# Second attention: the scores of both halves of the heads emitted ahead of their softmax, upper and lower rows of the array in turn

## The chip, the cores and the metric

The kernel runs on one core of a Trainium2 chip. The metric is the device time of one execution in microseconds (us); lower is better. TensorE is called PE in the profile, its weight loads PEld, VectorE DVE, ScalarE ACT, GpSimd POOL and SyncE SP.

## The reference, cut to what matters

Two blocks of two layers each run one after the other on 256 tokens of width 1024, in float32. The first block has two layers of a gated delta rule with an HGRN2 scan and a gated feed-forward network; the second has one layer of sparse attention and one of sliding-window attention, each followed by a convolutional feed-forward network. The change lies in the second attention alone, which is this:

```python
def swa_sink_mixer(h, k, v, w_q, sinks, w_out):
    ...
    sc = jnp.einsum('bnqgrd,bnkgd->bgrnqk', qb, kk).astype(jnp.float32) * (HEAD_DIM ** -0.5)
    ...
    sc = jnp.where(mask, sc, NEG)
    ...
    mx = jnp.maximum(sc.max(axis=-1, keepdims=True), sink)
    e = jnp.exp(sc - mx)
    p = e / (e.sum(axis=-1, keepdims=True) + jnp.exp(sink - mx))
    o = jnp.einsum('bgrnqk,bnkgd->bnqgrd', p.astype(vv.dtype), vv)
    return o.reshape(b, s, N_HEADS * HEAD_DIM) @ w_out
```

There are 16 query heads of 64 channels and 2 key heads. A query attends to the 128 positions up to its own. Each row of scores gets a learned sink value that takes part in the maximum and in the sum.

## The kernel before, in words

Activations lie channel by channel: partition p of chunk k is channel 128k+p, and the 256 tokens run along the free axis. Every large projection is three fp32r matmuls per weight tile (lines 185 to 187), on weights that ACT and DVE split in two as they arrive (lines 176 and 177).

The second attention is `_swa`. `SWA_ORDER` writes its steps out by hand: "q0 q1 q2 k0 u1 u3 q3 u0 u2 u5 u4 j0 u6 u7 j1 j2 j3". A "q" step projects four query heads, "k0" the keys and values, a "u" step is one unit of attention (`swa_unit`), a "j" step brings a quarter of the result back to channel-major form (`channel_major`, line 967), and `proj_out` follows.

There are eight units. Unit u(2n+c) takes four heads (two chunks r = 0, 1 of the query tile, and in each a lower half of the partitions, hf = 0, and an upper half, hf = 1) and the 128 queries of chunk c. Units with c = 1 (u1, u3, u5, u7) score 256 keys, those with c = 0 (u0, u2, u4, u6) 128. In what follows they are the wide and the narrow units. For one unit the code emits, for hf = 0 and then for hf = 1:

- a PSUM tile `sc` for the scores (line 1250, from `scores`, two buffers under the tag "sc") and two score matmuls, r = 0 and r = 1 (line 1252). They contract over 64 partitions, so each uses one half of the rows of the array; in float32 each is two passes in the trace, with a weight load each;
- the softmax in `softmax_rows`: two DVE instructions that add the mask and find the row maximum (line 951), two exponentials on ACT (through `act`, line 269), the transposes of the result through PE into a tile of the tag "px" (line 957; four for a wide unit, two for a narrow one, for each half), and one copy to `ptb` on ACT (line 959);
- the matmuls with the values into `po` (line 1257; four or two float32 matmuls for each half, two passes each). `po` has a single buffer.

After both halves come the sink's terms and the scaling into `ot` (lines 1259 to 1263).

The order in which instructions stand on an engine is not the order in which the code emits them. The build sorts them: an instruction is placed on its engine when, by the build's own plan, its inputs are there and its buffer is free, and among several that could go the one that was emitted first goes. So emission order is a priority. The trace shows this: scores of a later unit stand between the transposes of an earlier one.

The two lines that the change takes apart:

```python
for r in range(2):
    nc.tensor.matmul(sv[:, r * nk : (r + 1) * nk], q[a, 2 * n + r, c * P : (c + 1) * P], kt[a, 0, :nk], start=True, stop=True)
```

Of the kernel before, what the change touches and what calls it, by code (L numbers as in the profile page):

```python
# [16 lines left out]
P = 128  # L17
# [87 lines left out]
class K:  # L105
# [1136 lines left out]
    def swa_unit(self, n, c, q, kt, vv, nsk, ot):  # L1242
        nc = self.nc
        nk = (c + 1) * P
        sk = self.c("sink")
        st = self.sp.tile([P, 2, 8], F32, name="st", tag="st", bufs=4)
        po = self.psn.tile([P, 512], F32, name="po", tag="pn")
        for hf in range(2):
            a = slice(64 * hf, 64 * hf + 64)
            sv = self.scores()  # L1250
            for r in range(2):
                nc.tensor.matmul(sv[:, r * nk : (r + 1) * nk], q[a, 2 * n + r, c * P : (c + 1) * P], kt[a, 0, :nk], start=True, stop=True)  # L1252
            idx = [2 * r + hf for r in range(2)]
            ptb = self.softmax_rows(sv, self.c("bandcau") if c else self.c("cau"), [nsk[:, 4 * n + i : 4 * n + i + 1] for i in idx], st, idx, c)
            for r, u in enumerate(idx):
                for k in range(c + 1):
                    nc.tensor.matmul(po[:, 64 * u : 64 * u + 64], ptb[:, r * (c + 1) + k], vv[:, k, 64 * hf : 64 * hf + 64], start=k == 0, stop=k == c)  # L1257
        rr = self.sp.tile([P, 8], F32, name="rr", tag="rr", bufs=4)
        nc.vector.tensor_add(rr[:, :4], st[:, 0, :4], sk[:, 4 * n : 4 * n + 4])
        self.act(rr[:, :4], rr[:, :4], AF.Exp)  # L1260
        nc.vector.tensor_add(rr[:, :4], rr[:, :4], st[:, 1, :4])
        nc.vector.reciprocal(rr[:, 4:], rr[:, :4])
        nc.vector.tensor_mul(
            ot[:, c, n * 256 : (n + 1) * 256].rearrange("p (u d) -> p u d", d=64),
            po[:, :256].rearrange("p (u d) -> p u d", d=64),
            rr[:, 4:].rearrange("p (u o) -> p u o", o=1).to_broadcast([P, 4, 64]),
        )
# [175 lines left out]
```

## Time and profile before

| | |
|---|---|
| median of three runs | 1612.43 us (1607.37 to 1614.89) |
| the profiled execution | 1614.79 us, its span 1613.0 us |
| mean granted clock of TensorE | 0.987 of 2.4 GHz |
| PE busy | 1559.1 us, 97% of the span |
| DVE, ACT, POOL busy | 1191.5, 978.3 and 260.4 us (74%, 61%, 16%) |
| scores of the second attention (line 1252) | from 1351.6 to 1383 us of the span |

PE is busy nearly all the time, but a busy PE need not be a full one: matmuls are pipelined, the ends of their records are modelled, and waits inside the array count as busy. So the distance from one start to the next says more than the busy share. In the timeline a row merges instructions of one line that follow without a gap; the columns are start, length in us, engine, line, operation, tiles, shape and count, and in brackets the idle time before it with what ended it.

### The profile page before, as it was taken

How to read it: one execution, taken by the hardware profiler on the slowest of the kernel's cores; microseconds unless marked ns; L12 is line 12 of the kernel's file. 1: busy time of each engine (PE TensorE's matmuls, PEld its weight loads, DVE VectorE, ACT ScalarE, POOL GpSimd, SP SyncE). 2: the span in 40 equal slices, each digit the busy share in tenths (PEclk: the TensorE clock that was granted, in tenths of full speed). 3: DMA queues.
4: the chain of work that ended last, by engine and by line, in shares of the span. 5: the costliest groups of instructions: out<-in, count | busy, mean ns of one | idle time of the engine just before them, and what ended most of it. 6: DMA issues, size and time to landing. Idle time of an engine off the chain costs nothing.

```text
span 1613.0 us, 37688 instructions
## 1 busy us (share of the span) xinstructions
PE 1559.1 (97%) x15418; PEld 1497.6 (93%) x15418; DVE 1191.5 (74%) x2178; ACT 978.3 (61%) x1707; POOL 260.4 (16%) x243
## 2 busy tenths in 40 slices
PE   8999999999999989899999999999999999999997
PEld 8888889999999979789999998998999997999997
DVE  7795848777667885757777768786888667688853
ACT  7756755555546848574655554776666555666653
POOL 1021101122211201101122121003222100123210
PEclk9999999999999999999999999999999999999999
DMA  6542425566664532416655565532556654256562
GB/s 208 183 119 68 137 63 183 172 188 189 175 192 147 171 123 79 132 53 205 203 189 188 174 193 166 175 92 66 183 185 186 182 183 147 79 180 187 184 177 86
DMA packets 73436, 249.60 MB, mean 155 GB/s; under 512 B 10768, under 2 KB 11184, under 8 KB 73264
## 3 DMA queue, kind: packets, MB, share of 16 engines
q1 hardware_dynamic: 70752, 245.65, 49.1%
q8 instruction: 121, 1.98, 0.5%
q10 hardware_dynamic: 2512, 1.55, 0.3%
q14 instruction: 51, 0.42, 0.1%
HBM read 243.34 MB, written 1.06 MB: 152 GB/s over the span
## 4 chain that ended last, share of the span: by engine, by line
PE 48%; DVE 2%; ACT 1%; issue 1%; DMA 0%; POOL 0%; SPq 0%; ACTq 0%; DVEq 0%
PE pu L185 9%; PE pu L187 9%; PE pu L186 9%; PE pa L185 4%; PE pa L186 4%; PE pa L187 4%; PE po L1069 1%; PE ps L957 1%; PE po L185 1%; PE po L186 1%; PE po L187 1%; DVE wlo L177 1%; PE sc L1252 1%; PE po L1257 1%; ACT whi L176 1%
## 5 line engine op out<-in xcount | busy, mean ns | idle before, releaser
L176 ACT CAST whi<-raw 128x1024 fp32r<-128x1024 f32 (+1 forms) x462 | 475.5, 1034 | 435.1 <-PE pu L186 264.8
L177 DVE TENSOR_TENSOR wlo<-raw,whi 128x1024 fp32r<-128x1024 f32 (+1 forms) x462 | 564.7, 1226 | 180.1 <-ACT whi L176 179.1
L185 PE MATMUL pu<-xh,whi 128*128 128x256 f32 x2368 | 671.4, 284 | 8.7 <-issue 3.8
L187 PE MATMUL pu<-xh,wlo 128*128 128x256 f32 x2368 | 671.6, 284 | 5.0 <-DVE wlo L177 5.0
L186 PE MATMUL pu<-xl,whi 128*128 128x256 f32 x2368 | 670.9, 283 | 0.0
L185 PEld LDWEIGHTS pu<-xh,whi 128*128 128x128 f32 x2368 | 447.4, 189 | 12.4 <-issue 6.1
L187 PEld LDWEIGHTS pu<-xh,wlo 128*128 128x128 f32 x2368 | 447.9, 189 | 9.4 <-DVE wlo L177 6.0
L186 PEld LDWEIGHTS pu<-xl,whi 128*128 128x128 f32 x2368 | 448.2, 189 | 4.8 <-issue 3.3
L185 PE MATMUL pa<-ah,whi 128*128 128x256 f32 x704 | 197.1, 280 | 0.0
L186 PE MATMUL pa<-al,whi 128*128 128x256 f32 x704 | 196.7, 279 | 0.0
L187 PE MATMUL pa<-ah,wlo 128*128 128x256 f32 x704 | 196.7, 279 | 0.0
L186 PEld LDWEIGHTS pa<-al,whi 128*128 128x128 f32 x704 | 132.1, 188 | 0.0
L187 PEld LDWEIGHTS pa<-ah,wlo 128*128 128x128 f32 x704 | 132.0, 188 | 0.0
L185 PEld LDWEIGHTS pa<-ah,whi 128*128 128x128 f32 x704 | 132.0, 188 | 0.0
L360 POOL TENSOR_TENSOR sg<-sg,cu 128x256 f32<-128x256 f32 x44 | 71.6, 1628 | 196.5 <-DVE al L339 159.2
L360 POOL TENSOR_TENSOR sg<-sg,gu 128x256 f32<-128x256 f32 x44 | 61.1, 1388 | 204.1 <-ACT sg L269 204.1
L350 DVE TENSOR_TENSOR gu<-pu,rbc 128x512 f32<-128x512 f32 x88 | 60.8, 691 | 43.7 <-PE pu L187 43.7
L217 POOL TENSOR_TENSOR ssum<-ssum,sq 128x256 f32<-128x256 f32 x45 | 45.0, 1001 | 287.5 <-ACT sq L215 286.9
L265 ACT ACT_TABLE_LOAD x44 | 56.5, 1283 | 1.9 <-PEq L1435 1.2
L202 DVE SCALAR_TENSOR_TENSOR xl<-x,cst,xh 128x256 fp32r<-128x256 f32 x64 | 44.7, 724 | 3.6 <-ACT xh L201 3.5
L502 POOL TENSOR_TENSOR mt<-mt 128x512 f32<-128x512 f32 x8 | 12.3, 1536 | 199.5 <-DVE mt L500 199.5
L269 ACT ACTIVATE prb<-prb,st 128x256 f32<-128x256 f32 (+1 forms) x96 | 42.8, 449 | 1.9 <-DVE st L951 1.7
(388 smaller groups left out, 2437.0 us busy)
## 6 DMA issues: line engine op xcount, KB each, us to landing
raw<-in_up SPq DMA_DIRECT2D x176, 512.0 KB, 3.7
raw<-in_win SPq DMA_DIRECT2D x96, 512.0 KB, 3.6
raw<-in_dn SPq DMA_DIRECT2D x64, 512.0 KB, 3.6
raw<-in_dn SPq DMA_DIRECT2D x32, 384.0 KB, 3.2
raw<-in_wout SPq DMA_DIRECT2D x16, 512.0 KB, 3.8
raw<-in_awin SPq DMA_DIRECT2D x16, 512.0 KB, 4.0
raw<-in_whi SPq DMA_DIRECT2D x8, 512.0 KB, 3.6
raw<-in_wbd SPq DMA_DIRECT2D x8, 512.0 KB, 4.5
```

The costliest lines, as they stand in the source:

```text
L176: self.split = [nc.scalar.copy(hi[:, :n], raw[:, :n])]
L177: nc.vector.tensor_sub(lo[:, :n], raw[:, :n], hi[:, :n].bitcast(F32))
L185: nc.tensor.matmul(out, a, xh[:, k0 + k, :], start=first and k == 0, stop=False)
L186: nc.tensor.matmul(out, a, xl[:, k0 + k, :], start=False, stop=False)
L187: nc.tensor.matmul(out, b, xh[:, k0 + k, :], start=False, stop=last and k == kc - 1)
L202: nc.vector.scalar_tensor_tensor(self.xl[:, k, :], x, w, self.xh[:, k, :].bitcast(F32), ALU.mult, ALU.subtract)
L217: self.sum_on.tensor_add(self.acc[s][0], self.acc[s][0], sq)
L265: head = sc.preload_act_table(func)
L269: ins = sc.activation(out, in_, func, **kw)
L350: nc.vector.tensor_mul(gu, pt.rearrange("p (o t) -> p o t", o=2), self.rbc2())
L360: nc.gpsimd.tensor_mul(sg, sg, up)
L957: nc.tensor.transpose(pt[:, m * P : (m + 1) * P], pr[:, m * P : (m + 1) * P], self.c("ident"))
```

## The change

It allocates both score tiles of a unit at its start and emits the four score matmuls ahead of both softmaxes, with the halves in turn: r = 0 for hf = 0 and 1, then r = 1 for hf = 0 and 1. Then the softmax, transposes and value matmuls follow half by half as before. No instruction is added or taken away, and the number of buffers stays two.

```diff
-        for hf in range(2):
+        svs = [self.scores() for _ in range(2)]
+        for r in range(2):
+            for hf in range(2):
+                a = slice(64 * hf, 64 * hf + 64)
+                nc.tensor.matmul(svs[hf][:, r * nk : (r + 1) * nk], q[a, 2 * n + r, c * P : (c + 1) * P], kt[a, 0, :nk], start=True, stop=True)
+        for hf, sv in enumerate(svs):
             a = slice(64 * hf, 64 * hf + 64)
-            sv = self.scores()
-            for r in range(2):
-                nc.tensor.matmul(sv[:, r * nk : (r + 1) * nk], q[a, 2 * n + r, c * P : (c + 1) * P], kt[a, 0, :nk], start=True, stop=True)
             idx = [2 * r + hf for r in range(2)]
```

## Rows read from the trace of the kernel before

**Rows 1.** The page: busy time by engine, and the chain by line.
```profile
PE 1559.1 (97%) x15418; PEld 1497.6 (93%) x15418; DVE 1191.5 (74%) x2178; ACT 978.3 (61%) x1707; POOL 260.4 (16%) x243
...
PE pu L185 9%; PE pu L187 9%; PE pu L186 9%; PE pa L185 4%; PE pa L186 4%; PE pa L187 4%; PE po L1069 1%; PE ps L957 1%; PE po L185 1%; PE po L186 1%; PE po L187 1%; DVE wlo L177 1%; PE sc L1252 1%; PE po L1257 1%; ACT whi L176 1%
```

**Rows 2.** Windows: us, busy PE, PEld, DVE, ACT, POOL, then clock, DMA share, GB/s.
```profile
1351.60:1388.00 36.40, 35.28 (x226) 26.18 (x226) 22.07 (x102) 24.91 (x91) 0.00 (x0) 1.00 0.17 57
```

**Rows 3.** Groups by line and shape from 1351 to 1392 us: the scores.
```profile
L1252 PE MATMUL sc<-kt,q 64*128 64x256 f32 x32 | 9.5, 422 | 1.1 <-DVE st L951 1.1
...
L1252 PE MATMUL sc<-kt,q 64*128 64x128 f32 x32 | 6.3, 316 | 0.0
```

**Rows 4.** Waits of PE from 1351.6 to 1388 us: the only one, total, times, longest.
```profile
PE sc L1252 <- DVE st L951: 1.1, 1, 1.1
```

**Rows 5.** Timeline of PE around the wide units u1 and u3.
```profile
1351.62 1.14 PE L1252 MATMUL sc<-kt,q 64*128 64x256 f32 x8
1353.87 0.70 PE L1252 MATMUL sc<-kt,q 64*128 64x256 f32 x2 [1.11 <-DVE st L951]
1354.50 0.66 PE L957 MATMUL ps<-cst,prb 128*128 128x128 f32 x4
1355.09 0.70 PE L1252 MATMUL sc<-kt,q 64*128 64x256 f32 x2
1355.71 0.44 PE L957 MATMUL ps<-cst,prb 128*128 128x128 f32 x2
1356.08 0.70 PE L1252 MATMUL sc<-kt,q 64*128 64x256 f32 x2
1356.71 1.10 PE L1257 MATMUL po<-vv,ptb 128*128 128x64 f32 x8
...
1357.97 0.70 PE L1252 MATMUL sc<-kt,q 64*128 64x256 f32 x2
1358.59 0.44 PE L957 MATMUL ps<-cst,prb 128*128 128x128 f32 x2
```

**Rows 6.** Timeline of PE around the narrow units u0 and u2.
```profile
1360.63 0.49 PE L1252 MATMUL sc<-kt,q 64*128 64x128 f32 x4
1361.06 0.44 PE L957 MATMUL ps<-cst,prb 128*128 128x128 f32 x2
...
1363.10 0.49 PE L1252 MATMUL sc<-kt,q 64*128 64x128 f32 x2
...
1363.78 0.48 PE L1252 MATMUL sc<-kt,q 64*128 64x128 f32 x2
1364.19 0.33 PE L957 MATMUL ps<-cst,prb 128*128 128x128 f32 x1
1364.45 0.71 PE L1252 MATMUL sc<-kt,q 64*128 64x128 f32 x4
1365.09 1.10 PE L1257 MATMUL po<-vv,ptb 128*128 128x64 f32 x8
```

**Rows 7.** Timeline of PE where transposes follow each other with no score between.
```profile
1385.25 0.38 PE L967 MATMUL ps<-cst,ot 128*128 128x128 f32 x2
1385.47 0.38 PE L957 MATMUL ps<-cst,prb 128*128 128x128 f32 x2
```

**Rows 8.** Timeline of PE, windows under 0.1 us: first passes of two stretches.
```profile
1351.62 0.49 PE L1252 MATMUL sc<-kt,q 64*128 64x256 f32 x2
...
1360.63 0.38 PE L1252 MATMUL sc<-kt,q 64*128 64x128 f32 x2
```

**Rows 9.** Timeline of DVE and ACT: reads of u1's scores, then softmax of u3.
```profile
1353.33 0.48 DVE L951 CUSTOM_DVE_ANT_0 prb<-sc,cst,nsk 128x256 f32<-128x256 f32 x1
...
1354.14 0.48 DVE L951 CUSTOM_DVE_ANT_0 prb<-sc,cst,nsk 128x256 f32<-128x256 f32 x1
...
1355.82 0.48 DVE L951 CUSTOM_DVE_ANT_0 prb<-sc,cst,nsk 128x256 f32<-128x256 f32 x1
...
1356.35 0.51 ACT L269 ACTIVATE prb<-prb,st 128x256 f32<-128x256 f32 x1
```

## The prediction

> **What bounds the kernel now.** I read the page first: PE is busy 97% of the span, and the chain that ended last is nearly all matmuls of the projections; the scores of the second attention hold 1% of it and the value matmuls another 1% [rows 1]. So the change touches one short stage. The window over it says how short: the eight units take 36.4 us, in which PE is busy for 35.3, ACT for 24.9, DVE for 22.1, at the full clock throughout [rows 2]. The scores are busy for 9.5 + 6.3 = 15.8 us of it [rows 3], and that is all that packing can touch: removing them altogether would be 1.0% of the kernel. The list of waits of PE has one entry in that stage, 1.1 us at the first score of the second unit, which waits for a score buffer [rows 4]. PE's own order of work sets the end here, and the other two engines have room.
>
> The timeline shows what PE does in the stage. The first unit's four score matmuls stand together, eight passes; after that the scores of a unit stand alone or in twos, between transposes and value matmuls of the unit before [rows 5, 6]. Over the stage I count 25 stretches: one of eight passes, four of four, twenty of two. A lone score is dear: a wide one lasts 0.62 us to the next instruction's start (1355.09 to 1355.71), and the two transposes behind it take 0.37 (1355.71 to 1356.08) [rows 5], where two transposes that follow transposes take 0.22 [rows 7]. So leaving the half array and going back to it costs 0.15 us besides, and a lone wide score costs 0.62 + 0.15 = 0.77. The narrow one: 0.41 (1363.78 to 1364.19), and 0.15 again from the single transpose of 0.26 behind it, where 0.11 is usual; 0.56 together [rows 6, 7].
>
> **What packing is worth, and that it is there already.** Four passes of narrow scores take 0.43 us at 1360.63 and 0.64 at 1364.45 [rows 6]: the first are of two halves and run side by side, the second are of one half and follow each other. The eight wide passes of u1 take 1.14 us [rows 5], where even two of the four, one behind the other, would take 2 × 0.62 = 1.24; a window of 0.05 us holds the starts of two passes, there and at 1360.63 [rows 8]. The code emits u1's scores one half after the other, so passes of two halves share the array as soon as they are neighbours in PE's queue; they need not be emitted in turn. The Trainium skill, "TensorE: Matmul & The Clock Gate", Part 3, under "What overlaps and what doesn't", says that matmuls start and end in strict order, without reordering; by that, emitting in turn would be what lets them share, and the sum would be that of the first rival below. The trace disagrees in u1, and the forecast goes by the trace.
>
> **The change part by part.** It removes and adds no instruction, no DMA and no buffer; nothing moves past the queues of SP or POOL. It changes the priority of one score in each unit, the first of the upper half, which now goes ahead of the second of the lower half, and it puts both upper scores ahead of the lower half's softmax and transposes.
>
> 1. *Where they stand together (u1).* All four were together and shared the array. Their order changes, their time does not: 0.
>
> 2. *Where they fill gaps (the other seven units).* These scores stand where PE would otherwise wait for an exponential or a copy of the unit before, which was emitted earlier and goes first when ready. The change does not touch that: the unit before still has priority over all four scores. So I expect the same 25 stretches with the second and third score changed about: 0 for the twelve lone wide scores and the eight lone narrow ones.
>
> 3. *The second buffer.* An upper score can go second only if its buffer is free. Buffers come free half by half: u1's lower half is read until 1353.7 and its upper half from then to 1354.6, 0.81 us apart (the starts 1353.33 and 1354.14 of the two last reads) [rows 9]. That is why I don't expect first scores of both halves as neighbours: when the first buffer is free a score is placed at once. The second score of u3 starts at 1355.09 [rows 5], by which time both buffers are free, so it can be an upper one with no new wait: 0. Bounds: 0 below, as a wait cannot gain; above, 0.81 for each wide unit but u1, if PE is held for it.
>
> 4. *The stretches of four.* Two of them (u2 and u6) are now the two upper scores, at 0.64; in turn, third and fourth are one of each half and cost 0.43, so 2 × 0.21 = 0.42 us gained. The other two (u0 and u4) are second and third score, of two halves either way: 0.
>
> 5. *The lower softmax starts a score later.* Its inputs were scores one and two, they become one and three. For u3 that is 1356.08 in place of 1355.09, 0.99 us [rows 5]. DVE then starts it at about 1356.8 in place of 1355.82, and the exponential, now 1356.35 to 1356.86, ends near 1357.85 [rows 9]; the transposes that want it start at 1358.59 [rows 5]. The cover is 1.73 us of value matmuls and transposes of u1, and 0.7 of it is left: cost 0. If the cover were gone: 0.99 for each of the three wide units, and for u2 and u6 0.67 (1363.78 to 1364.45) [rows 6], 4.3 us together. The upper half's softmax wants score four as before. What is late next is the copy on ACT behind it, which still has the same matmuls ahead.
>
> The sum is −0.4 us, on the profiled execution 1614.8 to 1614.4. That execution is 2.4 us above the median of the three runs, so the forecast is 1612.4 − 0.4 = **1612.0 us**: no change that can be told. A measurement of this kernel tells about 0.5%, 8 us, from no change; the runs shown lie 7.5 us apart.
>
> **The rivals.**
>
> *Pairs form.* The build places the first scores of both halves together and then the second ones. For it: the emission asks for just that, and at 1360.63 a pair stands already. Against it: the buffers come free 0.81 us apart, and gaps are filled one score at a time. A wide pair would cost 0.62 + 0.02 (the narrow pair's 0.43 against 0.41) + 0.15 = 0.79, a narrow one 0.43 + 0.15 = 0.58. Three wide units go from 4 × 0.77 = 3.08 to 1.58, 4.5 us gained; u0 and u4 from 0.56 + 0.58 + 0.56 to 1.16, 1.1 gained; u2 and u6 from 0.56 + 0.56 + 0.79 to 1.16, 1.5 gained. Together 7.1 us: **1605.3**.
>
> *All four together, as in u1.* If the priority lets a unit's scores go as a block, a wide unit costs 1.14 − 0.08 (a record outlasts the next start by that) + 0.15 = 1.21, a narrow one 0.43 + 0.23 (two more passes, 0.64 − 0.41) + 0.15 = 0.81. Gains: 3 × 1.87 + 2 × 0.89 + 2 × 1.10 = 9.6 us: **1602.8**. Against it is the same, more strongly; it is also the most that the change can give, as ACT's 24.9 us would then fill nearly all of the 26.8 that are left.
>
> *The late lower softmax is not covered.* Place: the transposes of each unit's lower half. Price: 4.3 us as above, less 0.4: **1616.3**. It decides once the exponential ends after its transposes could start, that is once the 0.7 us left in u3 are used up, for instance if ACT gets the two halves' exponentials at once behind a copy. For it: DVE and ACT would work in bursts, where now they are served by turns. Against it: the slack above, and PE's single wait. If the second buffer's 0.81 us were waited for as well, in seven units, it would be up to 5.7 us more: 1622.
>
> *It does nothing.* If gaps are filled the same way and only names change, also without the 0.4 us: 1612.4, inside the forecast.
>
> **How the numbers follow.** Forecast, nothing doing included, 0.60; pairs 0.16; blocks 0.06; late softmax 0.14; late softmax and buffer 0.04. Likeliest case alone: 1609 to 1615, the scatter of runs around it. The range takes in pairs below and the uncovered softmax above, with about a microsecond for scatter: **1604.5 to 1617.5**; blocks and the double wait lie outside. Only blocks pass 0.5% to the faster side (1604.4), and pairs with a low run: 0.09. Only the double wait does so to the slower side (1620.5): 0.04. Within 0.5%: 0.87.
>
> **What would show each step.** The scores' stretches in PE's timeline decide it. Forecast right: some 25 stretches from first to last score over about 31 us, mostly two passes, and the stretches of four at 0.43 us each. Pairs: about 15 stretches. Blocks: 8 of eight passes. Late softmax: new waits of PE's transposes for the exponentials, in the list of waits. The forecast would be wrong if the stage's span moved by over 2 us either way; if it stays and the kernel moves, the cause lies behind the stage, in how the build sorts the projection that follows.

## The result, and the profile after

The change costs time: 1631.49 us, median of four runs (1621.81 to 1643.45), against 1613.66 for the kernel before in runs taken in turn with it. The ratio is 1.0119, 95% interval 1.007 to 1.0168. The forecast was 1612.0, range 1604.5 to 1617.5: the measured time lies 14 us above the upper end, on the side that was given 0.04. The profiled execution took 1643.45 us, its span 1641.6; it is the slowest of the four, so what its trace loses is more than the 17.8 us between the medians.

The ratios leave out executions far above a kernel's own fastest; the medians are of all.

The mean granted clock of TensorE over a whole execution is near 0.985 in most executions of this document and near 0.970 in others, and each row of the table below counts those under 0.98 (51 us at half clock in a span of 1640 take 0.016 off the mean). In what follows "kept" and "lost" of executions without a trace mean this count. It is no proof: every profiled execution has other stretches at half clock outside the second attention, 29 to 65 us together, so a mean of 0.976 to 0.981 can be either. Of the change's four executions three were under 0.98 (0.965, 0.968, 0.970). The fastest, at 0.981, still took 1621.8 us, 4 us above the range, and no trace tells what it lost.

The page of the profiled execution gives the first hint. PE is 25 us busier, with the same 15418 instructions as in [rows 1], and the row of the granted clock has a dip, 5 and 7, at slices 34 and 35 of 40.

The page after: busy times, and the clock in tenths by slices.
```profile
PE 1584.3 (97%) x15418; PEld 1515.2 (92%) x15418; DVE 1190.4 (73%) x2178; ACT 978.5 (60%) x1707; POOL 260.5 (16%) x243
...
PEclk9999999999999989899999999999999995799999
```

The windows over those slices tell where it begins and ends (columns as in [rows 2]).
```profile
1353.00:1356.00 3.00, 3.00 (x28) 3.00 (x27) 1.81 (x3) 1.38 (x2) 0.00 (x0) 1.00 0.46 114
1356.00:1360.00 4.00, 1.74 (x14) 1.16 (x13) 3.70 (x9) 1.58 (x4) 0.00 (x0) 1.00 0.79 257
1360.00:1364.00 4.00, 4.00 (x17) 2.35 (x17) 1.62 (x9) 2.52 (x10) 0.00 (x0) 0.79 0.81 249
1364.00:1368.00 4.00, 4.00 (x16) 2.47 (x16) 1.72 (x8) 2.00 (x7) 0.00 (x0) 0.50 0.10 36
...
1408.00:1412.00 4.00, 4.00 (x16) 3.02 (x16) 1.69 (x9) 1.96 (x7) 0.00 (x0) 0.50 0.00 0
1412.00:1416.00 4.00, 4.00 (x29) 3.74 (x28) 1.01 (x6) 1.56 (x5) 0.00 (x0) 0.81 0.00 0
1416.00:1420.00 4.00, 3.92 (x34) 3.74 (x33) 2.17 (x4) 1.77 (x4) 0.00 (x0) 1.00 0.00 0
...
1356.50:1418.60 62.10, 59.77 (x241) 43.37 (x240) 22.60 (x103) 25.72 (x92) 0.00 (x0) 0.59 0.10 33
```
The stage in the kernel before:
```profile
1351.60:1389.10 37.50, 36.38 (x235) 27.28 (x235) 22.53 (x103) 25.49 (x92) 0.00 (x0) 1.00 0.17 55
```
The clock is 1.00 to the end of the projection, TensorE idles for more than half of the next 4 us, and in the window from 1360 the clock drops to 0.50, 1.2 GHz. There it stays through nearly the whole of the attention, with PE busy all the time, and comes back at 1413.5, 3.2 us behind the first matmul of the output projection. The last row is the whole stage, from the start of the first score to the start of the last of the transposes back to channel-major form: 62.1 us. The same stretch took 37.5 us before (1351.6 to 1389.1, at full clock). These 24.6 us are the loss in the profiled execution. The two profiled spans differ by 28.6 us: the change's stage also began 4.9 us later, where the two programs are the same instruction by instruction, so that is scatter, and what follows it took 0.9 less.

The groups of PE from 1356 to 1419 us show it as duration: every kind of matmul is longer, not only the scores that the change touches (scores 594 and 494 ns, where [rows 3] have 422 and 316; value matmuls 401 where that window of before has 278).
```profile
L1259 PE MATMUL po<-vv,ptb 128*128 128x64 f32 x96 | 22.1, 401 | 0.1
L957 PE MATMUL ps<-cst,prb 128*128 128x128 f32 x48 | 15.3, 404 | 0.0
L1252 PE MATMUL sc<-kt,q 64*128 64x256 f32 x32 | 13.3, 594 | 2.3 <-DVE st L951 2.3
L1252 PE MATMUL sc<-kt,q 64*128 64x128 f32 x32 | 11.5, 494 | 0.0
```

What was different before the clock fell? The first eight passes take 1.14 us as before. Then the one idle gap of the stage, 1.1 us in [rows 4, 5], is 2.26. Timeline of PE after:
```profile
1356.50 1.14 PE L1252 MATMUL sc<-kt,q 64*128 64x256 f32 x8
1359.89 0.70 PE L1252 MATMUL sc<-kt,q 64*128 64x256 f32 x2 [2.26 <-DVE st L951]
1360.52 0.66 PE L957 MATMUL ps<-cst,prb 128*128 128x128 f32 x4
1361.11 0.70 PE L1252 MATMUL sc<-kt,q 64*128 64x256 f32 x2
1361.74 0.44 PE L957 MATMUL ps<-cst,prb 128*128 128x128 f32 x2
1362.11 1.04 PE L1252 MATMUL sc<-kt,q 64*128 64x256 f32 x2
```
These rows are the rows of [rows 5], in the same order. The clock falls at 1362.3, in the last of them, when PE has begun 19 passes of the stage; its order first differs from that of before at the 32nd. So up to the fall the gap is the only difference on PE.

The releaser is DVE's read of the scores (line 951), so the next view is DVE's timeline, after and then before:
```profile
1357.22 0.68 DVE L939 TENSOR_TENSOR q<-pu,rq 128x512 f32<-128x512 f32 x1
1357.82 1.22 DVE L177 TENSOR_TENSOR wlo<-raw,whi 128x1024 fp32r<-128x1024 f32 x1
1358.95 0.48 DVE L951 CUSTOM_DVE_ANT_0 prb<-sc,cst,nsk 128x256 f32<-128x256 f32 x1
```
The same stretch of the kernel before:
```profile
1352.33 0.68 DVE L939 TENSOR_TENSOR q<-pu,rq 128x512 f32<-128x512 f32 x1
1352.93 0.47 DVE L951 CUSTOM_DVE_ANT_0 prb<-sc,cst,nsk 128x256 f32<-128x256 f32 x1
...
1354.54 1.22 DVE L177 TENSOR_TENSOR wlo<-raw,whi 128x1024 fp32r<-128x1024 f32 x1
```
Line 177 here is the split of the fourth output weight, which nothing in the attention needs. Before, it stood behind u1's four reads; now it stands ahead of them, and u3's first score, which wants a buffer that the second read frees, waits 1.15 us longer. DVE's order changed though no DVE instruction was touched. The reason may be the build's plan, in which u1's first softmax now needs the third score and so looks late enough for the split to go first. That is inferred from the order and from the first experiment; the plan's own times were not seen.

### The profile page after: what moved, and what is told of

Its sections match the earlier page's. It is cut to its first block, busy times and chain, and to the rows that moved or that the text cites. A ratio compares the mean times of both kernels' runs of the same rounds, so it can differ in the third digit from the quotient of the medians.

```text
span 1641.6 us, 37692 instructions
## 1 busy us (share of the span) xinstructions
PE 1584.3 (97%) x15418; PEld 1515.2 (92%) x15418; DVE 1190.4 (73%) x2178; ACT 978.5 (60%) x1707; POOL 260.5 (16%) x243
## 4 chain that ended last, share of the span: by engine, by line
PE 49%; DVE 2%; ACT 1%; issue 1%; DMA 0%; SPq 0%; ACTq 0%; DVEq 0%
PE pu L185 9%; PE pu L187 9%; PE pu L186 9%; PE pa L185 4%; PE pa L186 4%; PE pa L187 4%; PE ps L957 1%; PE sc L1252 1%; PE po L1259 1%; PE po L1069 1%; PE po L185 1%; PE po L186 1%; PE po L187 1%; ACT whi L176 1%; DVE wlo L177 1%; PE sc L1063 1%
## 5 line engine op out<-in xcount | busy, mean ns | idle before, releaser
L202 DVE SCALAR_TENSOR_TENSOR xl<-x,cst,xh 128x256 fp32r<-128x256 f32 x64 | 44.7, 724 | 3.6 <-ACT xh L201 3.5
```

The lines of the kernel that those rows point to most:

```text
L202: nc.vector.scalar_tensor_tensor(self.xl[:, k, :], x, w, self.xh[:, k, :].bitcast(F32), ALU.mult, ALU.subtract)
```

## The experiments

Theories in the order in which they came up: A, the one gap at the start of the stage costs the clock; B, the order of the scores does (lone scores on half the rows); C, chance, whatever the order; and for the last four runs D, TensorE's work in the stage is too thin, wherever and for whatever reason. In e9, f2 and f3 both halves' scores are emitted ahead of the softmax as in the change, but half by half as before; no run here has that emission without fillers. Runs with the same value in the column "before beside it" were made together; those beside 1607.8 ran on another chip than the other experiments. Summary, medians of all executions:

| run | what | us (n) | before beside it | ratio, 95% | mean clock under 0.98 |
|---|---|---|---|---|---|
| before | | | | | 4 of 60 |
| after | the change | 1631.5 (4) | 1613.7 | 1.0119 (1.007 to 1.0168) | 3 of 4 |
| e1 | in turn in u1 alone | 1638.6 (4) | 1613.0 | 1.0162 (1.01 to 1.0225) | 4 of 4 |
| e4 | before, split ahead | 1634.4 (4) | 1613.0 | 1.0163 (1.0111 to 1.0216) | 4 of 4 |
| e3 | change, split behind | 1618.5 (10) | 1613.0 | 1.0052 (1.0017 to 1.0088) | 4 of 10 |
| e5 | change, gap filled | 1619.0 (10) | 1613.0 | 1.004 (1.0002 to 1.0078) | 2 of 10 |
| e8 | change, both | 1638.5 (4) | 1616.5 | 1.0114 (1.0083 to 1.0146) | 4 of 4 |
| e9 | before, gap filled | 1630.1 (10) | 1616.5 | 1.0053 (1.0011 to 1.0096) | 9 of 10 |
| e7 | blocks | 1616.9 (10) | 1616.5 | 1.0009 (0.9984 to 1.0035) | 3 of 10 |
| e10 | blocks, split behind, filled | 1606.3 (4) | 1616.5 | 0.9919 (0.9895 to 0.9943) | 0 of 4 |
| f1 | change, all units filled | 1624.3 (6) | 1607.8 | 1.0111 (1.0062 to 1.016) | 0 of 6 |
| f2 | before, all units filled | 1612.4 (12) | 1607.8 | 1.0047 (1.0017 to 1.0076) | 0 of 12 |
| f3 | e9's kernel, one more execution | 1621.3 (1) | | | 1 of 1 |
| f4 | blocks, filled | 1603.5 (10) | 1607.8 | 0.9985 (0.9951 to 1.0019) | 1 of 10 |

### Which part of the change does it

e1: only u1 emits in turn.
```diff
+        turn = (n, c) == (0, 1)
+        svs = [self.scores() for _ in range(2)] if turn else [None, None]
...
+        if turn:
+            for r in range(2):
+                for hf in range(2):
+                    score(hf, r)
```


> Only u1's scores in turn, the other seven units as before; DVE again splits the weight ahead of u1's softmax. Theory A: gap of 2.2 to 2.3 us ahead of u3's first score, clock 0.50 in most of the stage, 1620 to 1643. Theory B: seven of eight units have the old order, so clock 1.00 and 1611 to 1617. Theory C: scatter over both.

Measured 1638.6 us, the clock lost in all four. The gap in its trace is 2.26 us again, the clock 0.50 from 1360.3 to 1411.5 us:
```profile
1357.93 0.70 PE L1253 MATMUL sc<-kt,q 64*128 64x256 f32 x2 [2.26 <-DVE st L951]
...
1360.30:1411.40 51.10, 51.10 (x182) 37.45 (x183) 16.20 (x86) 19.82 (x77) 0.00 (x0) 0.50 0.04 16
```
When it fell, PE had begun 19 passes of the stage, in the order of before. One unit is enough; the other seven are not needed for the loss.

e4: the emission of before, and u1's first read queued behind the split. Nothing else of the program is changed.
```diff
-            nc.vector.tensor_sub(lo[:, :n], raw[:, :n], hi[:, :n].bitcast(F32))
+            self.ahead_of(nc.vector.tensor_sub(lo[:, :n], raw[:, :n], hi[:, :n].bitcast(F32)))
...
+    def ahead_of(self, ins):
+        if getattr(self, "hold", None):
+            first = self.hold.pop(0)
+            if first:
+                self.queue(first, ins)
```


> The kernel before with its emission, half by half, where only u1's first softmax read is queued on DVE behind the split of the fourth output weight. Theory A: gap of 2.2 to 2.3 us, clock 0.50 in most of the stage, 1620 to 1643 although no score is in turn. Theory B: clock 1.00, at most the 1.15 us of the later softmax, 1612 to 1618. Theory C: scatter.

Measured 1634.4 us, the clock lost in all four. Its PE timeline has the gap, its windows the clock:
```profile
1337.56 1.14 PE L1255 MATMUL sc<-kt,q 64*128 64x256 f32 x8
1340.95 1.22 PE L1255 MATMUL sc<-kt,q 64*128 64x256 f32 x2 [2.25 <-DVE st L951]
```
```profile
1337.50:1340.50 3.00, 1.20 (x10) 0.71 (x8) 2.83 (x6) 1.05 (x1) 0.00 (x0) 1.00 0.78 281
1340.80:1348.80 8.00, 7.85 (x24) 4.91 (x24) 2.90 (x14) 3.89 (x15) 0.00 (x0) 0.50 0.46 150
...
1364.80:1398.60 33.80, 33.80 (x121) 24.77 (x122) 10.28 (x52) 12.89 (x49) 0.00 (x0) 0.50 0.00 0
```
With no score emitted elsewhere, the place of a single 1.22 us DVE instruction gives the whole loss. The build does sort PE's work anew behind it: from the 31st pass of the stage on the order is another than before, and it is that of e1 pass by pass. But the clock falls at 1340.7, within the gap, when PE has run only the first unit's eight passes. So B is not needed for the loss here, nor in the change and in e1.

e3: the change, and the split queued behind the last of u1's reads.
```diff
+            self.behind(nc.vector.tensor_sub(lo[:, :n], raw[:, :n], hi[:, :n].bitcast(F32)))
...
+        self.hold = [None] * 3 + [self.first_red]
```


> The change in all eight units, but the split of the fourth output weight is queued on DVE behind u1's last softmax read, where it stood before. Theory A: gap of about 1.1 us, clock 1.00 through the stage, 1611 to 1617. Theory B: clock 0.50 in the stage, 1622 to 1643. Theory C: scatter.

Measured 1618.5 us, 13 us less than the change; the clock was kept in six of ten executions, the profiled one among them:
```profile
1350.98 0.70 PE L1253 MATMUL sc<-kt,q 64*128 64x256 f32 x2 [1.12 <-DVE st L951]
```
```profile
1348.70:1387.60 38.90, 37.65 (x239) 27.87 (x239) 22.54 (x103) 25.47 (x92) 0.00 (x0) 1.00 0.16 52
```
The gap is back at 1.12 us, and at full clock the stage in turn takes 38.9 us against 37.5: 1.4 us, in one profile of each, are the price of the order itself. Theory A's 1611 to 1617 was missed by a little. And four of ten against 4 of 60 for the kernel before says that with the same gap the clock is lost more often; where it fell in those four no trace shows. The gap is not all.

e5: the change, and three matmuls that serve nothing behind u1's scores, to fill the gap.
```diff
+        if (n, c) == (0, 1):
+            for i in range(3):
+                nc.tensor.matmul(po[:, S:], kt[:, 0, :P], kt[:, 0], start=True, stop=True)
```


> The changed kernel with three float32 matmuls of 128x256 more, behind u1's scores, into the unused half of u1's value tile; nothing else differs on any engine. Theory A, the gap: DVE splits a weight (1.22 us) ahead of u1's first softmax, so PE stands idle for 2.26 us in place of 1.11 ahead of u3's first score, TensorE's clock falls to half behind that gap and stays there for the rest of the stage. Then with the gap filled (under 1.2 us of it left) the stage runs at a granted clock of 1.00, lasts some 38 us and the time is 1611 to 1617. Theory B, the order: the scores standing one by one among the transposes let the clock fall wherever the gap is: stage at 0.50, 1622 to 1643 as the change. Theory C, chance: the clock falls in some executions of either kernel: the times of this one scatter between 1610 and 1640.

Measured 1619.0 us, the clock lost in two of ten; in the profile the gap left is 0.76 us and the stage 39.5 us at full clock. That is again above A's 1611 to 1617. Up to here A stood well, apart from e3's four and these two.

### Where A falls

e8 puts e3 and e5 together, so that no gap should be left.

> The change in all units with both remedies: the split behind u1's softmax and three matmuls more in the gap. PE then stands still for well under 0.5 us ahead of u3's first score. Theory A, the gap alone: clock 1.00 in the stage in every execution, 1610 to 1616, the stage some 39 us from first score to last transpose. Theory B, the order has its own share: clock 0.50 in the stage of a few executions in ten, times up to 1640.

Measured 1638.5 us, the clock lost in all four. The first gap is gone, but the second softmax now sits in another place, and a new gap has opened further in. Timeline of PE and windows of e8:
```profile
1359.92 2.00 PE L1265 MATMUL po<-vv,ptb 128*128 128x64 f32 x16
1361.85 0.70 PE L1253 MATMUL sc<-kt,q 64*128 64x256 f32 x4
1363.53 0.48 PE L1253 MATMUL sc<-kt,q 64*128 64x128 f32 x2 [0.98 <-DVE st L951]
```
```profile
1354.40:1362.50 8.10, 7.99 (x48) 5.30 (x46) 5.57 (x16) 4.29 (x12) 0.00 (x0) 1.00 0.73 249
1362.50:1364.00 1.50, 0.52 (x5) 0.35 (x3) 1.42 (x7) 0.89 (x3) 0.00 (x0) 1.00 0.05 14
1364.20:1380.00 15.80, 15.80 (x51) 10.68 (x50) 4.57 (x30) 5.79 (x25) 0.00 (x0) 0.50 0.00 1
```
The clock falls at 1364.1, right behind a gap of 0.98 us, shorter than the 1.11 that the kernel before has and survives [rows 4, 5]. What stood around it differs: ahead of it 16 value passes of 64 columns and two wide scores (four passes) side by side, behind it one narrow score (two passes). PE's order is another than that of before from the ninth pass on, so here the order may have its share.

e9 emits the scores half by half, as the kernel before, with the three fillers behind u1's.

> The order of the kernel before with the same three matmuls in its gap of 1.11 us. Theory A: the gap is closed, the stage keeps 1.00, and nothing else changes but up to 0.3 us of PE time: 1607 to 1615, and fewer high times than the kernel before has. Theory C, chance: as many high times as before, the same median.

Measured 1630.1 us, the clock lost in nine of ten, where the kernel before alone loses it in 4 of 60. The gap ahead of u3's first score is closed, and it made things worse; A cannot say that. But e9 is not only the kernel before with a gap filled: the build also puts u1's six transposes ahead of u3's first score, as the timeline of f3, the same kernel, shows:
```profile
1344.88 1.56 PE L1255 MATMUL po<-kt 128*128 128x256 f32 x6
1346.30 1.42 PE L957 MATMUL ps<-cst,prb 128*128 128x128 f32 x6
1347.65 0.70 PE L1252 MATMUL sc<-kt,q 64*128 64x256 f32 x2
```
So fillers and a new order were tried together.

e7 sends the four scores of each unit as one block: one tile of two banks in place of two buffers, and the scores at high priority.
```diff
+        both = self.psc.tile([P, 2, 512], F32, name="sc", tag="sc", bufs=1)
+        svs = [both[:, hf] for hf in range(2)]
+        with self.tc.high_priority():
...
```


> The four scores of each unit stand together: one tile of two banks in place of two tiles, so a unit's scores wait until both halves of the unit before are read, and they have priority. The split is ahead of u1's softmax again and nothing fills the gap, which is longer (3 us or more, as PE's first work behind u1's scores is its transposes). Theory A: clock 0.50 in most of the stage, 1620 to 1640 in spite of 8 stretches of scores for 25. Theory B, by which lone scores among the transposes are what lets the clock fall: clock 1.00 and some 9 us gained, about 1604.

Measured 1616.9 us beside 1616.5, which neither theory gave (1620 to 1640, and 1604); the clock lost in three of ten. In the profiled execution the stage is at full clock, PE waits 3.3 us for exponentials, one of the waits, right behind u1's scores, 2.5 us long and longer than that of the change, and yet the clock holds:
```profile
PE ps L957 <- ACT prb L269: 3.3, 2, 2.5
```
So a long gap does not always lose the clock, and no gap does not always keep it. What e7 has and the runs before it have not are scores of both halves side by side in all units: they are busy for 4.5 + 2.9 = 7.4 us of its stage, against 15.8 in [rows 3].

### What takes the place of A

D was then put to a test that A cannot pass: more work for TensorE, spread over the stage.

f3 first, e9's kernel once more, for the place where its clock falls: e9's own profiled execution kept it, with a stage of 38.6 us.

> The order of the kernel before with three passes behind the first unit's scores once more, for a look at where its clock is lost, which its profiled execution did not show (its nine others, of ten, had a mean granted clock of 0.97). Theory D: the fall begins not behind the first unit, where TensorE is now never idle, but further in, 6 us or more behind the first score, in a stretch of value passes and single scores. If the filler passes themselves were what loses the clock, it falls within 4 us of the first score. Mean granted clock 0.97 and a span of 1630 us if it falls, 0.98 and 1610 us if this execution keeps it.

```profile
1343.80:1350.00 6.20, 6.09 (x37) 4.06 (x36) 4.45 (x14) 4.10 (x12) 0.00 (x0) 1.00 0.73 223
...
1353.00:1356.30 3.30, 3.04 (x20) 2.25 (x18) 1.21 (x8) 2.44 (x10) 0.00 (x0) 1.00 0.00 0
1356.30:1364.30 8.00, 8.00 (x26) 5.35 (x24) 2.60 (x17) 3.31 (x14) 0.00 (x0) 0.50 0.00 1
```
It falls at 1356.3, 12.5 us behind the first score, as D expected. Ahead of it PE was busy for 3.04 of 3.30 us, 92%. The groups of those 3.3 us show with what:
```profile
L1252 PE MATMUL sc<-kt,q 64*128 64x128 f32 x6 | 1.5, 322 | 0.0
L957 PE MATMUL ps<-cst,prb 128*128 128x128 f32 x6 | 1.3, 303 | 0.0
L1262 PE MATMUL po<-vv,ptb 128*128 128x64 f32 x8 | 1.1, 281 | 0.3 <-ACT ptb L959 0.3
```
Three narrow scores on half the rows (six passes), each standing alone, six transposes, eight value passes of 64 columns, and 0.26 us of idle time. No long gap stood ahead of this fall, and a busy share of 92% did not keep the clock. Which of these passes, or which order of them, let it go, no row shows.

f2: the kernel before with three fillers behind u1's scores, as e9, and two behind those of each other unit.
```diff
-        if (n, c) == (0, 1):
-            for i in range(3):
+        for i in range(3 if (n, c) == (0, 1) else 2):
```


> The order of the kernel before, with the same passes: three behind the first unit's scores (that alone lost the clock in nine executions of ten and took 1630.1 us), and two behind those of each of the other seven units. Theory D: the fourteen further passes thicken the rest of the stage, and the clock is kept: mean granted clock about 0.983, 1616 + 1.1 + up to 3.0 = 1617 to 1620 us, so faster than with three passes although it does more. If the three passes behind the first unit do the harm by themselves (they put the second unit's scores 1.5 us later), the clock is still lost in most executions and the time is 1630 to 1634 us.

The clock was kept in all twelve. Median 1612.4 us beside 1607.8: 4.6 us over the kernel before, where e9 was 13.6 over it. The program differs from e9's by 14 added matmuls (28 passes) and in how the build sorts around them; e9 ran on another chip, but f3, the same kernel as e9, lost the clock in its one execution on this one; f2's stage is 5.8 us longer at full clock (44.4 against 38.6), and beside its own kernel before it is faster. Its timeline at the place where e9 fell has dense passes in front of the value passes:
```profile
1352.82 1.13 PE L1254 MATMUL po<-kt 128*128 128x256 f32 x4
1353.79 1.00 PE L1261 MATMUL po<-vv,ptb 128*128 128x64 f32 x8
```
```profile
1343.10:1387.60 44.50, 44.24 (x276) 34.25 (x274) 22.86 (x103) 25.95 (x92) 0.00 (x0) 1.00 0.14 47
```

f1: the same fillers in the change itself.

> The change as it stands, with whole-array fp32 passes of 256 columns that serve nothing (the keys by themselves, into the half of each unit's output tile that nothing reads): three behind the scores of the first unit, as in the kernel with the gap filled, and two behind those of each of the other seven; nothing of the computation is left out. Theory D (new): TensorE's clock is lost wherever the second attention's own work is too thin for some microseconds, whether by an idle gap, by scores on half the rows or by value passes of 64 columns spread out; then more work on TensorE keeps the clock: mean granted clock about 0.983 in nine executions of ten, and the time is the full-clock time of the change plus the fillers, 1613.7 + 1.4 + up to 17 x 0.22 = 3.7 us, 1616 to 1619 us, against 1631.5 of the change. Theory A (the one gap at the start, which three fillers close): nothing is won over the kernel with the gap filled alone, 1619 + 14 x 0.22 = 1622 us, with the clock lost in two executions of ten as there. Theory C (chance, no bearing of the order): the share of executions with the clock lost is anything.

The clock was kept in all six, against one in four for the change, with the split still ahead. This does not tell D from A: the first unit's fillers leave a gap of 0.77 us, as in e5 (0.76), and e5 without the other units' fillers kept the clock in eight of ten. The time is a miss: 1624.3 us beside 1607.8, where D had 1616 to 1619 and A 1622. Of the 16.5 us, 7.2 are in the stage (44.7 against 37.5), because I had counted one pass for each filler and float32 takes two: 34 passes, 9.1 us busy, start to start 0.216.
```profile
L1254 PE MATMUL po<-kt 128*128 128x256 f32 x34 | 9.1, 391 | 0.0
```
The other 9 us do not show in the stage; in the profiled executions the stage starts 3.9 us later than in that of before and what follows it takes about the same. Why this kernel's six executions are all that late stays open.

### Blocks with fillers

e10 is e7 with four fillers behind u1's scores and the split queued behind its reads; f4 is e10 without the queue.

> The blocks with both remedies. What the prediction's rows made of blocks is 9.6 us at full clock, less 0.2 to 0.5 for the four matmuls more; with the clock held the stage should last 28 to 31 us from u1's first score to the last transpose in place of 37.5, and the time be about 1604. If the chain of softmax binds once PE has less to do, the stage lasts 33 us or more and PE shows new waits for ACT.

> All four scores of a unit in one stretch into one tile of two banks, with four filler passes behind the first unit's, and the split of the fourth output weight where the build puts it. With that split queued behind as well, this took 1606.3 us (ratio 0.9919); without filler and queue 1616.9. Theory D: the passes over both row halves at once and the first products of the output projection that the build now puts into the stage keep TensorE's work thick, so the clock is kept in nearly all executions; the split's 1.22 us delays the first softmax once: 1606.3 + 1.2 = 1607.5 us, ratio 0.990 to 0.995. Theory A: the split opens the first gap again by 1.2 us beyond the four fillers' 0.86 us, and the clock is lost in some executions: 1612 us or more, ratio above 0.997.

e10: 1606.3 us, ratio 0.9919 (0.9895 to 0.9943), the only version with its interval below 1, in four executions; the clock kept in all four. Its stage, and its scores:
```profile
1354.50:1387.50 33.00, 31.72 (x253) 26.34 (x251) 22.20 (x103) 25.07 (x92) 0.00 (x0) 1.00 0.19 62
```
```profile
L1255 PE MATMUL sc<-kt,q 64*128 64x256 f32 x32 | 4.5, 402 | 0.0
L1255 PE MATMUL sc<-kt,q 64*128 64x128 f32 x32 | 2.9, 297 | 0.1
```
The scores are busy for 7.4 us in place of 15.8 [rows 3], and the stage takes 32.8 us in place of 37.5 although 2.0 us of fillers (8 passes) are in it. Of the two cases that were expected it is nearly the second, 33 us with new waits for ACT: PE waits 0.9 us for ACT's copies, and ACT's 25.1 us are now three quarters of the stage. The stage gives 4.7 us; the medians differ by 10.2. The clock does not explain the rest, as the kernel before beside it lost it in none of 18: the remaining 5.5 us are not explained.

f4: 1603.5 us beside 1607.8, ratio 0.9985 (0.9951 to 1.0019), not told from no change. D expected 0.990 to 0.995 and A above 0.997, so the ratio came out on A's side, while the clock was kept in nine of ten, as D had it (the tenth, at 0.977 and 1608.8 us, can be either). The stage is 36.2 us, at full clock in the profile: without the queue PE idles for 3.3 us of it where e10's idles for 1.3, 1.4 of it in a new wait for exponentials. The queue is worth more than the split's own 1.22 us that was allowed for it.

## Why the prediction was wrong

*The step that failed* stands in the first part: "at the full clock throughout" [rows 2]. Every duration of the sum was taken at 2.4 GHz, and none of the rivals let that change. In the profiled execution the missing term is nearly the whole loss: stage 62.1 us in place of 37.5, 23 us of it the clock (62.1 against the 38.9 and 39.5 of e3 and e5, in which it was kept).

*Step 1, u1 together: 0.* Right for PE: eight passes in 1.14 us as before. What it left out is DVE. The step looked at the time of the scores and not at which score the first softmax waits for in the build's plan. Step 5 asked that for u3 and for the other units behind it, where matmuls cover it, and not for u1, where nothing does; and it did not ask what else DVE could be given in the meantime, such as the split that stands behind the four reads, 1.22 us long. By the rule stated ahead of the prediction, that emission order is a priority among what is ready, it could have been found. Even so it would have been costed at 1.15 us, one longer gap, since the clock was not in the sum.

*Step 2, the same stretches.* Right in the count: 25 stretches of scores in PE's timeline after, as the 25 before. They are not all the same ones: of the four stretches of four narrow passes two are left, and two others now hold four passes that share the array, one of two units and one of two wide scores. Pairs or blocks throughout did not form.

*Step 3, no wait for the second buffer.* Right: PE's only wait in the stage is still that of u3's first score.

*Step 4, 0.42 us gained, and step 5, 0 for the late softmax.* The sum of them, −0.4, was measured without the clock by e3: +1.4 us in the stage. The wide scores are busy for 9.5 us as before, the narrow ones for 7.0 in place of 6.3, so half of what was lost lies in the narrow scores, where step 4 saw the gain: two of their stretches of four came apart. That is within the 2 us which the text allowed the stage.

*The rivals.* None had it. The late softmax had the right sign and the right engine but the wrong unit, and 4.3 us is not 18. Blocks were rejected as something that emission alone would not do, and rightly. Made by a tile of two banks they take 8.4 us of busy time off the scores, but the stage, for which 9.6 us were estimated, gave 1.3 (e7, 36.2 us) and 4.7 (e10): part of PE's time became waits for ACT.

*What the text offered as a test* served: the stage's span moved by over 2 us, and that is where the loss was.

The runs show the following, then. The split's place is enough for the loss (e4), u1 in turn is enough for the split's place (e1), and taking it back returns most executions (e3). What a gap does to the clock is not settled by its length (e7, e8, e9). With more work on TensorE in all units the clock was kept in 18 of 18 executions (f1, f2), with the split ahead as well as behind; f2 beside e9 and f3 speaks for D, which is supported by that and not shown. The kernel before loses its clock too, in 4 of 60. What stays open is why that one lasts so well with its gap of 1.11 us where e3, with 1.12 and the scores in turn, loses it in four of ten, though PE's order is the same for the first 31 passes of the stage; and since the build also sorts anew around the fillers, work and order were not tried apart in e8, e9, f1 and f2.

The Trainium skill, "TensorE: Matmul & The Clock Gate", Part 1, "HAM oscillation — how this bites in real kernels", puts the loss down to idle gaps of PE, there waits for DMA of some 3 to 5 us. The losses here came behind shorter ones: 2.26 us in the change, 0.98 in e8, 0.26 in f3; and e7's profiled execution held through 2.5.

## What to carry to other kernels

A stage made of scores on half the rows, transposes and narrow value passes can have PE busy nearly all the time (92% ahead of the fall in f3) and still lose TensorE's clock, and in the five profiled losses it came back only behind the first matmuls of the output projection: so look at the granted clock of the stage first, of several executions, and then at the gaps and the work in it. Before an emission order is costed at nothing, ask for every engine which input of its next instruction now comes later in the build's plan, and which ready instruction could go first. And one gap filled need not help, as e8 and e9 show: here the clock was kept with fillers in every unit (f1, f2), at a cost of some 7 us in the stage, and by blocks with fillers (e10, f4), of which only e10 came out faster than the kernel before, by 0.8% in four executions.

## What the runs showed of the hardware that was not expected

- At half clock PE is busy 100% of the time in the attention (windows of the change from 1364 to 1412 us) and the clock does not return; in all five profiled losses it returned 3 to 6 us behind the first matmul of the output projection (at 1413.5 us in the change, 1411.5 in e1, 1398.7 in e4, 1411.9 in e8 and 1397.3 in f3).
- The same program keeps the clock in one execution and loses it in the next: the stage of e9's profiled execution is at 1.00 throughout and takes 38.6 us, that of f3, the same kernel, falls to 0.50 at 1356.3 us.
- Adding 28 passes of 256 columns to a kernel (e9 to f2) brought it from 13.6 to 4.6 us over the kernel before that ran beside it.
